# A decoder layer in fp32: five of 22 weight pieces of each half of the down projections as seven block products, and turns queued behind the weight split

## The chip, the cores and the metric

The kernel runs on one core of a Trainium2 chip. The time is device microseconds of that core, from launch to end; the measure is the median of several runs. A profile of one execution gives each instruction of the engines: TensorE (PE, and PEld for its weight loads), VectorE (DVE), ScalarE (ACT), GpSimd (POOL) and SyncE (SP), which issues most DMAs.

## The reference

One hybrid decoder layer on 256 tokens of width 2048, all in float32:

```python
def swiglu(h, w_gu, w_down):
    gate, up = jnp.split(h @ w_gu, 2, axis=-1)
    return (jax.nn.silu(gate) * up) @ w_down

x = x + 0.5 * swiglu(rmsnorm(x, ffn1_norm[l]), ffn1_w_gu[l], ffn1_w_down[l])   # D_FF = 5632
z = rmsnorm(x, mix_norm[l]) @ w_in[l]
... sliding-window attention and an HGRN2 recurrence on columns of z ...
x = x + merged @ w_out[l]
x = x + 0.5 * swiglu(rmsnorm(x, ffn2_norm[l]), ffn2_w_gu[l], ffn2_w_down[l])
```

The change bears on the two products with `w_down`, (256 x 5632) @ (5632 x 2048).

## The kernel before

**Products.** fp32 precision is made from three products of a reduced type: each operand is split into a high part (a copy to fp32r) and a low part (the rest), and hi x hi, hi x lo and lo x hi are summed. All weights stream through as *pieces* of 128 x 2048 elements (1 MB), in one list, `plan`. For each piece `load_next` issues its DMA on SP into one of four `w_raw` buffers, and `split_next` makes `w_hi` on ScalarE (line 154) and `w_lo` on VectorE (line 155) into one of two buffers each. `take` hands out piece i and first splits up to piece i + 1; a `w_hi` buffer comes free when TensorE is done with piece i - 1. A piece holds two row blocks of 128 times 1024 columns, or the like, and is used for both token halves (t = 0, 1): 8 blocks of 512 columns, each three matmuls.

**Seven products.** From group `first` on, the gate/up stage of an FFN computes two of the eight pieces of a group (`Seven.KCS = (1, 4)`) with a Strassen-like scheme: seven block products of three matmuls. It needs sums of the four weight blocks (`sums`, VectorE, lines 434 to 436, from `w_raw`), their split (`parts`: `T_hi` on ScalarE, `T_lo` on VectorE, lines 440 and 441), sums of the activation blocks (`forms`, lines 421 to 428) and two sets of four PSUM banks: `plain` takes what belongs to one output block, `summed` what is shared by several. `share` adds the shared ones up into `e`, and `outputs` adds `plain` to them. A seven-product piece needs `w_lo` for three of its four blocks only (1536 columns). The down projections are plain.

**Turns.** An activation is transposed by `send` and `fetch`: VectorE transposes 32 x 32 blocks into a block buffer (line 360), POOL's queue writes it to DRAM (line 362), and four DMAs on POOL's queue read it back with the blocks in place (line 372). Block buffers come from pool `t2` (six slots of 128 x 512); the tiles read back from `s4` (22 slots of 128 x 1024) or `t2`. `put_turned` splits a turned tile into the halves that the down projections read (`f_ah` on ScalarE, line 384; `f_al` on VectorE, line 385).

**Order.** A planner lays out each engine's queue ahead of time, in the order in which its own durations let instructions start, earlier ones in the program first; a pool's slots are given out in program order. `tc.issue_after(ins)` puts an instruction behind `ins` on the same engine. `run_gap` runs the extra work of a piece (`gaps`) with such an edge behind the newest `w_lo` (`last["rest"]`). `tick`, called twice a piece, runs the next entry of the list `deferred`, and `flush` runs what is left at a stage's end.

**Down projections.** An FFN has F = 5632 = 11 groups of 512 columns (*quads*). The output is made in two halves of 1024 columns (`cg`), each 22 pieces; quad q of the activation serves pieces 2q and 2q + 1 of both halves and is fetched three quads ahead. In piece 0 of the first half `finish_last` finishes the last gate/up group: four additions (line 507), two gated parts (519, 521), two turns. At a half's end `project_residual` adds 0.5 times the four banks to `old`, the residual, loaded earlier (line 620), and `done` stores the result and, in the first FFN, starts the next norm (`h2`). `po`, the last projection before the second FFN, does the same for `h3`. For the first two quarters, `add_later` puts into `deferred`: the squares and the turn of the quarter, eight empty entries, and two `take_back`, which multiply the turned tile by the gains (line 279) and split it.

Of the kernel before, what the change touches and what calls it, by code (L numbers as in the profile page):

```python
# [15 lines left out]
P = 128  # L16
D = 2048
S = 256
# [38 lines left out]
def tile_layer(  # L57
# [11 lines left out]
    wp = ctx.enter_context(tc.tile_pool(name="wp", bufs=2))  # L69
    hp = ctx.enter_context(tc.tile_pool(name="hp", bufs=1))  # L70
    s4p = ctx.enter_context(tc.tile_pool(name="s4p", bufs=22))
    t2p = ctx.enter_context(tc.tile_pool(name="t2p", bufs=6))
    cp = ctx.enter_context(tc.tile_pool(name="cp", bufs=1))
    sp = ctx.enter_context(tc.tile_pool(name="sp", bufs=2))
    mmp = ctx.enter_context(tc.tile_pool(name="mmp", bufs=6, space=bass.MemoryType.PSUM))
# [5 lines left out]
    def t2(name, shape=(P, 512)):  # L81
        return t2p.tile(list(shape), F32, name=name, tag="t2")
# [152 lines left out]
    class Normed:  # L235
# [31 lines left out]
        def add_later(self, q, pieces):  # L267
            turned = []

            def turn_off():  # L270
                self.squares(q, pieces)
                turned.extend([fetch(x) for x in [send(self.name, pieces[t]) for t in range(T)]])

            def take_back(t):
                k = q * 4
                x, tok = turned[t], slice(t * P, (t + 1) * P)
                h, l = (y[:, k:k + 4, tok].rearrange("p q (g c) -> p g q c", g=4) for y in (self.hi, self.lo))
                with tc.issue_after(last["copy"]), tc.issue_after(last["rest"]):
                    VE.tensor_tensor(out=x, in0=x, in1=self.g[:, k:k + 4].unsqueeze(1).unsqueeze(3)
                                     .broadcast_to([P, 4, 4, 32]), op=ALU.mult)  # L280
                    SC.copy(h, x)
                    VE.tensor_tensor(out=l, in0=x, in1=h.bitcast(F32), op=ALU.subtract)

            if q < 2:

                deferred.extend([turn_off] + [nothing] * 8 + [lambda t=t: take_back(t) for t in range(T)])
                return

            def first():
                self.squares(q, pieces)  # L290
# [15 lines left out]
        def xh(self, k):  # L306
            return self.hi[:, k, :]
# [46 lines left out]

    def send(name, nat):

        blocks = t2(f"{name}_blk", (P, 4, 4, 32))
        VE.transpose(out=blocks, in_=nat.rearrange("p (q j i) -> p j q i", q=4, j=4))  # L360
        there = tc.dram_tile([P, 512], F32, name=f"{name}_dram")
        GP.dma_start(there, blocks.rearrange("p j q c -> p (j q c)"))  # L362
        return name, there
# [38 lines left out]
    class Seven:  # L402
# [14 lines left out]
        def forms(self, p):  # L417

            k = 2 * self.KCS[p]
            A, f = t2("A", (P, 2, S)), t2("S", (P, 4, P))  # L420
            VE.tensor_tensor(out=A, in0=self.h.hi[:, k:k + 2, :].bitcast(F32),
                             in1=self.h.lo[:, k:k + 2, :].bitcast(F32), op=ALU.add)
            a11, a21, a12, a22 = (A[:, j, t * P:(t + 1) * P] for j in (1, 0) for t in range(2))
            for i, x, y, op in ((0, a21, a22, ALU.add), (1, f[:, 0], a11, ALU.subtract),
                                (2, a21, a11, ALU.subtract), (3, a12, f[:, 1], ALU.subtract)):
                VE.tensor_tensor(out=f[:, i], in0=x, in1=y, op=op)
            SC.copy(self.sh[:, p], f)
            VE.tensor_tensor(out=self.sl[:, p], in0=f, in1=self.sh[:, p].bitcast(F32), op=ALU.subtract)

        def sums(self, i):  # L430

# [8 lines left out]
                SC.copy(h, t)  # L440
                VE.tensor_tensor(out=l, in0=t, in1=h.bitcast(F32), op=ALU.subtract)  # L441

        def project(self, plain, summed, gaps):

            h = self.h
            for kc in range(KT // 2):
                hi, lo = take(f"{self.name}_gu")
                run_gap(gaps, kc)
                k = 2 * kc
                if kc not in self.KCS:  # L450
                    for t in range(T):
                        tok = slice(t * P, (t + 1) * P)
                        order = [((0, 1), [i]) for i in range(2)] if kc == KT // 2 - 1 else \
                            [([j], range(2)) for j in range(2)]
                        for js, bs in order:
                            for j in js:
                                ah, al = h.xh(k + j)[:, tok], h.xl(k + j)[:, tok]
                                st, sp_ = kc == j == 0, kc == KT // 2 - 1 and j == 1
                                cols = {i: slice(j * 1024 + i * 512, j * 1024 + i * 512 + 512) for i in bs}
                                for i in bs:  # L460
                                    mm(plain[2 * t + i], ah, hi[:, cols[i]], st, False)
                                    mm(plain[2 * t + i], ah, lo[:, cols[i]], False, False)
                                for i in bs:
                                    mm(plain[2 * t + i], al, hi[:, cols[i]], False, sp_)
                        tick()
                    continue
                p = self.KCS.index(kc)

                def a(j, t):
                    return tuple(x(k + j)[:, t * P:(t + 1) * P] for x in (h.xh, h.xl))  # L470

                def s(i):
                    return self.sh[:, p, i], self.sl[:, p, i]

                def b(i):
                    return tuple(x[:, i * 512:(i + 1) * 512] for x in (hi, lo))

                def t(i):
                    c = slice(i % 2 * 512, i % 2 * 512 + 512)
                    return self.th[i // 2][:, c], self.tl[i // 2][:, c]  # L480

                for n, (o, x, y) in enumerate((
                        (plain[0], a(0, 0), b(0)), (plain[1], s(3), b(1)), (plain[2], a(0, 1), t(3)),
                        (summed[0], a(1, 0), b(2)), (summed[1], s(0), t(1)), (summed[2], s(1), t(2)),
                        (summed[3], s(2), t(0)))):
                    st, sp_ = n > 2 and p == 0, n > 2 and p == 1
                    mm(o, x[0], y[0], st, False)
                    mm(o, x[0], y[1], False, False)
                    mm(o, x[1], y[0], False, sp_)
                    if n in (2, 6):  # L490
                        tick()
# [17 lines left out]
    def ffn(name, h, old, done, first):  # L509
# [30 lines left out]
        base = taken[0]  # L540
        for g in range(first, G):
            seven.update(base + g * 8 + kc for kc in Seven.KCS)
        sets = None
        for g in range(G):
            gaps = {kc: [] for kc in range(8)}
# [32 lines left out]
            sets = [x[1], x[0]] if (G - 1 - g) % 2 == 0 else [x[0], x[1]]  # L578
            summed = sets[1]
            gaps[5].append(lambda: sv[0].share(summed))  # L580
            sv[0].project(sets[0], summed, gaps)

        def finish_last():
            sv[0].outputs(sets[0])
            for t in range(T):
                gated_part(G - 1, t, sv[0].e[t][:, :512], sv[0].e[t][:, 512:])
                send_part(G - 1, t)

        for cg in range(2):
            gaps = {kc: [] for kc in range(2 * G)}  # L590
            if cg == 0:
                gaps[0].append(finish_last)
            for q in range(G):
                Q = cg * G + q
                gaps[2 * q].append(lambda Q=Q: fetch_quad(Q + 3))
                for t in range(T):
                    gaps[2 * q + t].append(lambda Q=Q, t=t: put_quad(Q + 1, t))

            class Side:
                xh = staticmethod(lambda k, o=4 * G * cg: act.xh(o + k))  # L600
                xl = staticmethod(lambda k, o=4 * G * cg: act.xl(o + k))

            project_residual(f"{name}_d", cg, F // P, Side, 0.5, old, done, gaps)

    def project_residual(name, cg, nk, parts, scale, old, done, gaps={}):
# [11 lines left out]
        bk = project(name, 1024, nk, parts.xh, parts.xl, fetch, gaps)  # L617
# [687 lines left out]
```

## Time and the profile before

| | |
|---|---|
| median of 3 runs | 2081.43 us (2080.98, 2081.43, 2084.72) |
| profiled execution: time, span | 2085.7 us, 2083.9 us |
| busy: PE, PEld, DVE, ACT, POOL | 2069.9, 1709.2, 1396.1, 987.3, 306.7 us |
| matmuls (PE instructions) | 9369 |
| HBM read | 428.21 MB, 217 GB/s read and written over the span |

The profile's times are measured from the span's first instruction. Matmuls overlap in the records, so PE's busy time is an upper view of its work. A row of a timeline has the start, the duration of the merged instructions, the engine, the line, the operation and, in brackets, the idle time before it and what ended it.

### The profile page before, as it was taken

How to read it: one execution, taken by the hardware profiler on the slowest of the kernel's cores; microseconds unless marked ns; L12 is line 12 of the kernel's file. 1: busy time of each engine (PE TensorE's matmuls, PEld its weight loads, DVE VectorE, ACT ScalarE, POOL GpSimd, SP SyncE). 2: the span in 40 equal slices, each digit the busy share in tenths (PEclk: the TensorE clock that was granted, in tenths of full speed). 3: DMA queues.
4: the chain of work that ended last, by engine and by line, in shares of the span. 5: the costliest groups of instructions: out<-in, count | busy, mean ns of one | idle time of the engine just before them, and what ended most of it. 6: DMA issues, size and time to landing. Idle time of an engine off the chain costs nothing.

```text
span 2083.9 us, 24269 instructions
## 1 busy us (share of the span) xinstructions
PE 2069.9 (99%) x9369; PEld 1709.2 (82%) x9369; DVE 1396.1 (67%) x1344; ACT 987.3 (47%) x894; POOL 306.7 (15%) x550
## 2 busy tenths in 40 slices
PE   9999999999999999999999999999999999999999
PEld 7888888888878888878787888888888888888887
DVE  4877888886556565555576555567888788765554
ACT  5544444444445454444455533445444444544443
POOL 0011000014515000033120000101110000046400
PEclk9999999999999999999999999999999999999999
DMA  8576656668869665567354555776665666689963
GB/s 286 191 237 231 218 193 212 218 217 271 266 229 280 223 209 179 185 226 235 133 207 166 191 185 183 237 244 222 221 227 198 216 210 218 209 263 291 274 212 116
DMA packets 180122, 454.74 MB, mean 218 GB/s; under 512 B 18771, under 2 KB 21542, under 8 KB 180006
## 3 DMA queue, kind: packets, MB, share of 16 engines
q1 hardware_dynamic: 155830, 397.57, 56.5%
q0 software_dynamic: 20400, 48.79, 7.7%
q10 hardware_dynamic: 3776, 6.83, 1.0%
q8 instruction: 73, 1.20, 0.2%
q14 instruction: 43, 0.35, 0.0%
HBM read 428.21 MB, written 24.91 MB: 217 GB/s over the span
## 4 chain that ended last, share of the span: by engine, by line
PE 84%; issue 12%; DMA 2%; DVE 1%; ACT 0%; POOL 0%; POOLq 0%; DVEq 0%; ACTq 0%
PE P L94 38%; PE f_d L94 18%; PE f_gu L94 6%; PE zbA L94 4%; PE po L94 4%; PE zbR L94 4%; PE zgo L94 2%; PE pa L94 2%; PE pr L94 2%; DMA f_a_T<-f_a_dram 1%; DVE w_lo L155 1%; DMA h_T<-h_dram 1%; PE pv_ps L94 0%; PE o_ps L94 0%; PE s_ps L94 0%
## 5 line engine op out<-in xcount | busy, mean ns | idle before, releaser
L155 DVE TENSOR_TENSOR w_lo<-w_raw,w_hi 128x2048 fp32r<-128x2048 f32 (+2 forms) x374 | 826.4, 2211 | 579.2 <-ACT w_hi L154 578.8
L154 ACT CAST w_hi<-w_raw 128x2048 fp32r<-128x2048 f32 (+2 forms) x374 | 691.3, 1850 | 808.9 <-PE f_d L94 224.5
L94 PE MATMUL P<-w_lo,h_hi 128*128 128x512 f32 x988 | 384.2, 389 | 0.5 <-DVE w_lo L155 0.5
L94 PE MATMUL P<-w_hi,h_hi 128*128 128x512 f32 x988 | 383.9, 389 | 0.0
L94 PE MATMUL P<-w_hi,h_lo 128*128 128x512 f32 x988 | 322.7, 389 | 0.0
L94 PE MATMUL f_d<-w_lo,f_ah 128*128 128x512 f32 x704 | 274.7, 390 | 2.6 <-DVE w_lo L155 2.6
L94 PE MATMUL f_d<-w_hi,f_ah 128*128 128x512 f32 x704 | 274.7, 390 | 0.0
L94 PE MATMUL f_d<-w_hi,f_al 128*128 128x512 f32 x704 | 220.0, 390 | 0.0
L94 PEld LDWEIGHTS P<-w_lo,h_hi 128*128 128x128 f32 x988 | 185.4, 188 | 39.4 <-DVE w_lo L155 0.9
L94 PEld LDWEIGHTS P<-w_hi,h_lo 128*128 128x128 f32 x988 | 185.5, 188 | 38.4
L94 PEld LDWEIGHTS P<-w_hi,h_hi 128*128 128x128 f32 x988 | 185.5, 188 | 38.4
L372 POOL DMA_DIRECT2D f_a_T<-f_a_dram x352 | 191.6, 549 | 135.7 <-DMA f_a_T<-f_a_dram 51.0
L94 PEld LDWEIGHTS f_d<-w_lo,f_ah 128*128 128x128 f32 x704 | 132.6, 188 | 30.8 <-DVE w_lo L155 3.0
L94 PEld LDWEIGHTS f_d<-w_hi,f_ah 128*128 128x128 f32 x704 | 132.6, 188 | 27.4
L94 PEld LDWEIGHTS f_d<-w_hi,f_al 128*128 128x128 f32 x704 | 132.5, 188 | 27.5
L440 ACT CAST T_hi<-T 128x1024 fp32r<-128x1024 f32 x76 | 79.6, 1048 | 141.6 <-DVE T L434 140.0
L362 POOL DMA_DIRECT2D f_a_dram<-f_a_blk x44 | 24.3, 553 | 811.3 <-DVE f_a_blk L360 808.2
L441 DVE TENSOR_TENSOR T_lo<-T,T_hi 128x1024 fp32r<-128x1024 f32 x76 | 89.6, 1218 | 0.0
L94 PE MATMUL f_gu<-w_hi,h_hi 128*128 128x512 f32 x192 | 75.9, 397 | 0.7 <-ACT w_hi L154 0.7
L94 PE MATMUL f_gu<-w_lo,h_hi 128*128 128x512 f32 x192 | 74.8, 390 | 0.0
L94 PE MATMUL f_gu<-w_hi,h_lo 128*128 128x512 f32 x192 | 61.5, 390 | 0.0
L385 DVE TENSOR_TENSOR f_al<-f_a_T,f_ah 128x512 fp32r<-128x512 f32 x88 | 60.2, 684 | 0.0
(318 smaller groups left out, 2854.2 us busy)
## 6 DMA issues: line engine op xcount, KB each, us to landing
w_raw<-in_ffn_w_gu SPq DMA_DIRECT2D x350, 512.0 KB, 4.3
w_raw<-in_ffn_w_down SPq DMA_DIRECT2D x88, 1024.0 KB, 6.3
w_raw<-in_w_in SPq DMA_DIRECT2D x74, 1024.0 KB, 4.9
f_a_T<-f_a_dram POOLq DMA_DIRECT2D x352, 64.0 KB, 6.1
w_raw<-in_w_out SPq DMA_DIRECT2D x16, 1024.0 KB, 4.8
f_a_dram<-f_a_blk POOLq DMA_DIRECT2D x44, 256.0 KB, 5.3
w_raw<-in_w_attn_branch SPq DMA_DIRECT2D x8, 1024.0 KB, 4.8
w_raw<-in_w_hg_branch SPq DMA_DIRECT2D x8, 1024.0 KB, 4.8
```

The lines of the kernel that those rows point to most:

```text
L94: last["mm"] = PE.matmul(o, lhsT=lhsT, rhs=rhs, start=start, stop=stop).ins
L154: last["copy"] = SC.copy(hi[:, c], raw[:, c]).ins
L155: last["rest"] = VE.tensor_tensor(out=lo[:, c], in0=raw[:, c], in1=hi[:, c].bitcast(F32), op=ALU.subtract).ins
L362: GP.dma_start(there, blocks.rearrange("p j q c -> p (j q c)"))
L372: GP.dma_start(res[j * 32:(j + 1) * 32].rearrange("p g q c -> p g (q c)"), v[j])
L385: VE.tensor_tensor(out=l, in0=turned, in1=h.bitcast(F32), op=ALU.subtract)
L440: SC.copy(h, t)
L441: VE.tensor_tensor(out=l, in0=t, in1=h.bitcast(F32), op=ALU.subtract)
```

## The change

Pieces 3, 7, 11, 15 and 19 of the 22 of each half are computed as seven products. The forms come from the turned quad (`turned_forms`, a tile `Sd` in `s4`), three pieces ahead; `sums` two and `parts` one piece ahead. The two halves swap the roles of two sets of four banks, and the halves' ends are new: `share` in piece 20, `add_shared` (0.5 x shared + old, four VectorE instructions) in piece 21, and four final additions after it. `Seven.project` gets its operands as arguments. In `send` the block transpose is placed behind the newest `w_lo`, for every turn of the kernel; the blocks and turned tiles of `h2` and `h3` come from `s4`, and `t2` has seven slots.

```diff
-    t2p = ctx.enter_context(tc.tile_pool(name="t2p", bufs=6))
+    t2p = ctx.enter_context(tc.tile_pool(name="t2p", bufs=7))
@@ Normed.add_later
             def turn_off():
                 self.squares(q, pieces)
-                turned.extend([fetch(x) for x in [send(self.name, pieces[t]) for t in range(T)]])
+
+                blk, back = (s4(f"{self.name}_{n}", F32, (P, T, 4, 4, 32)) for n in ("blk", "T"))
+                there = [send(self.name, pieces[t], blk[:, t]) for t in range(T)]
+                turned.extend([fetch(x, back[:, t]) for t, x in enumerate(there)])
@@
-    def send(name, nat):
-
-        blocks = t2(f"{name}_blk", (P, 4, 4, 32))
-        VE.transpose(out=blocks, in_=nat.rearrange("p (q j i) -> p j q i", q=4, j=4))
+    def send(name, nat, blocks=None):
+
+        blocks = t2(f"{name}_blk", (P, 4, 4, 32)) if blocks is None else blocks
+        with tc.issue_after(last["rest"]):
+            VE.transpose(out=blocks, in_=nat.rearrange("p (q j i) -> p j q i", q=4, j=4))
@@ class Seven
+        def add_forms(self, a11, a21, a12, a22, hi, lo, view):
+            f = t2("S", (P, 4, P))
+            for i, x, y, op in ((0, a21, a22, ALU.add), (1, view(f[:, 0]), a11, ALU.subtract),
+                                (2, a21, a11, ALU.subtract), (3, a12, view(f[:, 1]), ALU.subtract)):
+                VE.tensor_tensor(out=view(f[:, i]), in0=x, in1=y, op=op)
+            SC.copy(hi, f)
+            VE.tensor_tensor(out=lo, in0=f, in1=hi.bitcast(F32), op=ALU.subtract)
+
+        def turned_forms(self, x, j):
+
+            r = s4("Sd", F32R, (P, 2, 4, P))
+            a11, a21, a12, a22 = (x[:, t, :, i, :] for i in (j + 1, j) for t in range(2))
+            self.add_forms(a11, a21, a12, a22, r[:, 0], r[:, 1], lambda y: y.rearrange("p (g c) -> p g c", g=4))
+            return r[:, 0], r[:, 1]
@@ ffn
+        KCD = range(3, 2 * G, 4)
+        for cg in range(2):
+            seven.update(base + G * 8 + cg * 2 * G + kc for kc in KCD)
...
+        last_plain = sets[0]
+        x = [bank("P") for _ in range(6)] + [trb("P") for _ in range(2)]
+        sets = [x[:4], x[4:]]
+        forms = {}
+
+        def make_forms(cg, kc):
+            forms[cg, kc] = sv[0].turned_forms(there[cg * G + kc // 2], 2 * (kc % 2))
 
         for cg in range(2):
             gaps = {kc: [] for kc in range(2 * G)}
             if cg == 0:
                 gaps[0].append(finish_last)
+            for kc in KCD:
+                gaps[kc - 3].append(lambda cg=cg, kc=kc: make_forms(cg, kc))
+                gaps[kc - 2].append(lambda i=base + G * 8 + cg * 2 * G + kc: sv[0].sums(i))
+                gaps[kc - 1].append(lambda: sv[0].parts())
             for q in range(G):
                 Q = cg * G + q
                 gaps[2 * q].append(lambda Q=Q: fetch_quad(Q + 3))
                 for t in range(T):
                     gaps[2 * q + t].append(lambda Q=Q, t=t: put_quad(Q + 1, t))
-            project_residual(f"{name}_d", cg, F // P, Side, 0.5, old, done, gaps)
+            plain, summed = sets[cg], sets[1 - cg]
+            res = []
...
+            def add_shared():
+                for t in range(T):
+                    for i in range(2):
+                        VE.scalar_tensor_tensor(out=res[i][t], in0=sv[0].e[t][:, i * 512:(i + 1) * 512], scalar=0.5,
+                                                in1=res[i][t], op0=ALU.mult, op1=ALU.add)
+
+            gaps[2 * G - 2].append(lambda: sv[0].share(summed))
+            gaps[2 * G - 1].append(add_shared)
+            sv[0].project(f"{name}_d", F // P, list(KCD), lambda k: act.xh(4 * G * cg + k),
+                          lambda k: act.xl(4 * G * cg + k), lambda kc: forms[cg, kc], plain, summed, gaps, fetch_old)
+            flush()
+            for t in range(T):
+                for i in range(2):
+                    VE.scalar_tensor_tensor(out=res[i][t], in0=plain[2 * t + i], scalar=0.5, in1=res[i][t],
+                                            op0=ALU.mult, op1=ALU.add)
+            for i in range(2):
+                done(cg * 2 + i, res[i])
```

`fetch_old` (left out) loads `old` as before, ahead of piece 19.

## Rows read from the trace of the kernel before

**Rows 1.** The page, busy time, share of the span, instructions.
```profile
PE 2069.9 (99%) x9369; PEld 1709.2 (82%) x9369; DVE 1396.1 (67%) x1344; ACT 987.3 (47%) x894; POOL 306.7 (15%) x550
```
**Rows 2.** The chain by time: start, duration, work.
```profile
618.89 15.07 PE f_d L94 x59
...
925.65 45.96 PE zgo L94 x191
...
1373.17 5.44 PE f_gu L94 x24
...
1840.22 239.44 PE f_d L94 x1056
```
**Rows 3.** Windows: busy time of each engine, granted clock, DMA share, GB/s.
```profile
611.00:630.00 19.00, 16.39 (x66) 13.05 (x65) 8.29 (x6) 8.16 (x10) 11.54 (x22) 0.91 0.80 240
...
921.00:971.00 50.00, 46.31 (x195) 37.84 (x193) 23.24 (x13) 23.99 (x24) 29.41 (x54) 0.93 0.85 279
...
1418.00:1840.00 422.00, 422.00 (x1863) 349.57 (x1862) 336.72 (x295) 200.13 (x151) 29.51 (x54) 1.00 0.64 217
```
**Rows 4.** TensorE's waits: total us, times, longest.
```profile
PE zgo L94 <- DVE w_lo L155: 3.7, 1, 3.7
PE f_d L94 <- DVE w_lo L155: 2.6, 1, 2.6
...
PE P L94 <- DVE w_lo L155: 0.5, 1, 0.5
```
**Rows 5.** VectorE's timeline, second half of the first FFN.
```profile
615.95 0.71 DVE L360 STREAM_TRANSPOSE h_blk<-old 128x512 f32<-128x512 f32 x1 [5.24 <-DMA h_dram<-h_blk]
```
**Rows 6.** VectorE's timeline, start of `zgo`.
```profile
922.00 1.43 DVE L360 STREAM_TRANSPOSE q0T_blk<-q 128x512 f32<-128x512 f32 x2 [4.17 <-DMA kT_dram<-kT_blk]
```
**Rows 7.** VectorE's groups by line and form: busy us, mean ns, idle before.
```profile
L155 DVE TENSOR_TENSOR w_lo<-w_raw,w_hi 128x2048 fp32r<-128x2048 f32 x330 | 754.9, 2288 | 555.4 <-ACT w_hi L154 555.1
L441 DVE TENSOR_TENSOR T_lo<-T,T_hi 128x1024 fp32r<-128x1024 f32 x76 | 89.6, 1218 | 0.0
L155 DVE TENSOR_TENSOR w_lo<-w_raw,w_hi 128x1536 fp32r<-128x1536 f32 x38 | 66.6, 1753 | 23.7 <-ACT w_hi L154 23.7
L385 DVE TENSOR_TENSOR f_al<-f_a_T,f_ah 128x512 fp32r<-128x512 f32 x88 | 60.2, 684 | 0.0
...
L434 DVE TENSOR_TENSOR T<-w_raw 128x1024 f32<-128x1024 f32 x38 | 45.7, 1202 | 0.0
...
L436 DVE TENSOR_TENSOR T<-w_raw,T 128x512 f32<-128x512 f32 x38 | 26.3, 692 | 1.3
...
L620 DVE SCALAR_TENSOR_TENSOR old<-f_d,old 128x512 f32<-128x512 f32 x16 | 10.6, 686 | 11.1 <-PE f_d L94 11.1
...
L426 DVE TENSOR_TENSOR S<-A 128x128 f32<-128x128 f32 x8 | 2.0, 288 | 0.1
```
**Rows 8.** VectorE's timeline, start of the second FFN's down projections.
```profile
1842.20 2.29 DVE L155 TENSOR_TENSOR w_lo<-w_raw,w_hi 128x2048 fp32r<-128x2048 f32 x1 [2.55 <-ACT w_hi L154]
1844.41 2.48 DVE L507 TENSOR_TENSOR E<-P,E 128x512 f32<-128x512 f32 x4
...
1848.70 2.25 DVE L155 TENSOR_TENSOR w_lo<-w_raw,w_hi 128x2048 fp32r<-128x2048 f32 x1
```
**Rows 9.** VectorE's timeline, last `po` project and start of `f_gu`.
```profile
1336.57 0.71 DVE L360 STREAM_TRANSPOSE h_blk<-old 128x512 f32<-128x512 f32 x1 [1.26 <-DMA x<-old]
...
1358.87 2.29 DVE L155 TENSOR_TENSOR w_lo<-w_raw,w_hi 128x2048 fp32r<-128x2048 f32 x1 [1.21 <-ACT w_hi L154]
...
1371.96 1.29 DVE L279 TENSOR_TENSOR h_T<-h_T,gains 128x512 f32<-128x512 f32 x2
...
1376.32 2.29 DVE L155 TENSOR_TENSOR w_lo<-w_raw,w_hi 128x2048 fp32r<-128x2048 f32 x1
```
**Rows 10.** POOL's timeline in `po`; landing times of the `h_T` fetches there.
```profile
1338.80 4.36 POOL L372 DMA_DIRECT2D h_T<-h_dram x8 [6.36 <-DMA h_dram<-h_blk]
...
DMA to landing us min/median/max: 4.2/7.1/7.8
```

More of the change, by code (lines that the diff above doesn't have):

```diff
@@ L419, in forms @@
             k = 2 * self.KCS[p]
-            A, f = t2("A", (P, 2, S)), t2("S", (P, 4, P))
+            A = t2("A", (P, 2, S))
             VE.tensor_tensor(out=A, in0=self.h.hi[:, k:k + 2, :].bitcast(F32),
@@ L423, in forms @@
             a11, a21, a12, a22 = (A[:, j, t * P:(t + 1) * P] for j in (1, 0) for t in range(2))
[L424 to L428, printed above, removed]
+            self.add_forms(a11, a21, a12, a22, self.sh[:, p], self.sl[:, p], lambda x: x)
+        def add_forms(self, a11, a21, a12, a22, hi, lo, view):
[10 more added lines that the diff above has]
+            return r[:, 0], r[:, 1]
         def sums(self, i):
@@ L441, in parts, with project @@
                 VE.tensor_tensor(out=l, in0=t, in1=h.bitcast(F32), op=ALU.subtract)
[L443 to L447, printed above, removed]
+        def project(self, name, nk, kcs, xh, xl, forms, plain, summed, gaps, near_end=None):
+            end = nk // 2 - 1
+            for kc in range(nk // 2):
+                hi, lo = take(name)
                 run_gap(gaps, kc)
                 k = 2 * kc
-                if kc not in self.KCS:
+                if kc == end - 2 and near_end is not None:
+                    near_end()
+                if kc not in kcs:
                     for t in range(T):
                         tok = slice(t * P, (t + 1) * P)
-                        order = [((0, 1), [i]) for i in range(2)] if kc == KT // 2 - 1 else \
+                        order = [((0, 1), [i]) for i in range(2)] if kc == end else \
                             [([j], range(2)) for j in range(2)]
@@ L456, in project @@
                             for j in js:
-                                ah, al = h.xh(k + j)[:, tok], h.xl(k + j)[:, tok]
-                                st, sp_ = kc == j == 0, kc == KT // 2 - 1 and j == 1
+                                ah, al = xh(k + j)[:, tok], xl(k + j)[:, tok]
+                                st, sp_ = kc == j == 0, kc == end and j == 1
                                 cols = {i: slice(j * 1024 + i * 512, j * 1024 + i * 512 + 512) for i in bs}
@@ L466, in project @@
                     continue
-                p = self.KCS.index(kc)
                 def a(j, t):
-                    return tuple(x(k + j)[:, t * P:(t + 1) * P] for x in (h.xh, h.xl))
+                    return tuple(x(k + j)[:, t * P:(t + 1) * P] for x in (xh, xl))
                 def s(i):
-                    return self.sh[:, p, i], self.sl[:, p, i]
+                    return tuple(x[:, i] for x in forms(kc))
                 def b(i):
@@ L485, in project @@
                         (summed[3], s(2), t(0)))):
-                    st, sp_ = n > 2 and p == 0, n > 2 and p == 1
+                    st, sp_ = n > 2 and kc == kcs[0], n > 2 and kc == kcs[-1]
                     mm(o, x[0], y[0], st, False)
@@ L580, in ffn @@
             gaps[5].append(lambda: sv[0].share(summed))
-            sv[0].project(sets[0], summed, gaps)
+            sv[0].project(f"{name}_gu", KT, Seven.KCS, h.xh, h.xl,
+                          lambda kc: [x[:, Seven.KCS.index(kc)] for x in (sv[0].sh, sv[0].sl)],
+                          sets[0], summed, gaps)
         def finish_last():
-            sv[0].outputs(sets[0])
+            sv[0].outputs(last_plain)
             for t in range(T):
@@ L597, in ffn, with fetch_old, project_residual @@
                     gaps[2 * q + t].append(lambda Q=Q, t=t: put_quad(Q + 1, t))
-            class Side:
-                xh = staticmethod(lambda k, o=4 * G * cg: act.xh(o + k))
-                xl = staticmethod(lambda k, o=4 * G * cg: act.xl(o + k))
-            project_residual(f"{name}_d", cg, F // P, Side, 0.5, old, done, gaps)
-    def project_residual(name, cg, nk, parts, scale, old, done, gaps={}):
+            plain, summed = sets[cg], sets[1 - cg]
+            res = []
+            def fetch_old():
+                for i in range(2):
+                    q = cg * 2 + i
+                    res.append([])
+                    for t in range(T):
+                        o = t2("old")
+                        nc.sync.dma_start(o, old[t * P:(t + 1) * P, q * 512:(q + 1) * 512])
+                        res[i].append(o)
+            def add_shared():
[8 more added lines that the diff above has]
+            flush()
+            for t in range(T):
+                for i in range(2):
+                    VE.scalar_tensor_tensor(out=res[i][t], in0=plain[2 * t + i], scalar=0.5, in1=res[i][t],
+                                            op0=ALU.mult, op1=ALU.add)
+            for i in range(2):
+                done(cg * 2 + i, res[i])
+    def project_residual(name, cg, nk, parts, scale, old, done):
         res = []
@@ L615, in fetch @@
                     res[i].append(o)
-        bk = project(name, 1024, nk, parts.xh, parts.xl, fetch, gaps)
+        bk = project(name, 1024, nk, parts.xh, parts.xl, fetch)
         for t in range(T):
```

## The prediction

> **What bounds the kernel now.** I read the page's busy shares first, then the chain by time and the windows, then TensorE's waits, and only then the timelines around the places that the change touches. TensorE is busy 99% of the span [rows 1], and that share alone says little, because matmuls overlap in it. The chain says more: in the second FFN's down projections 1056 matmuls start one after another in 239.44 us [rows 2], 0.2267 us each, and the gate/up stage before it passes 1863 in 422.0 us, again 0.2265 each [rows 3]. In that stage two of eight weight pieces already run as seven products; those products cost what any matmul costs, and nothing waits there. So nearly everywhere the time is the number of 512-column matmuls times 0.2267 us: a matmul taken out is worth that much as long as VectorE, which makes the low halves and the sums, keeps ahead.
>
> It doesn't keep ahead in two places [rows 4]: the first `zgo` piece waits 3.7 us for `w_lo`, and one down piece of the first FFN 2.6 us. Each has a tail: the granted clock is 0.91 and 0.93 in those windows instead of 1.00 [rows 3]. In the chain the 59 matmuls after the `f_d` wait take 15.07 us, 1.7 more than 59 x 0.2267, and the 191 after the `zgo` wait 45.96 us, 2.6 more [rows 2]. The waits thus cost 2.6 + 1.7 = 4.3 us and 3.7 + 2.6 = 6.3 us. Both have one cause. A turn's block transpose (L360) stands in VectorE's queue ahead of a split's `w_lo` and waits for its `t2` slot, held by an earlier block whose send is still under way: 5.24 us at 615.95 [rows 5], 4.17 us at 922.00 [rows 6].
>
> **The matmuls removed.** A plain piece is 8 block products of three matmuls, 24; a piece as seven products is 21. Five pieces in each of two halves in two FFNs are 20 pieces: 60 matmuls x 0.2267 = 13.6 us. I take it whole; the lower end, with each piece losing its three in waits, is nothing.
>
> **The two old waits.** Inside `send` the transpose now gets an edge behind the newest split that is traced, so the turn of h2's second quarter can no longer run far ahead of its place in the program, in front of a `w_lo`; h2's blocks also leave the `t2` slots. The same edge spreads the twelve `kT`, `qT`, `q0T` turns over the ticks at which they are traced, two a piece of 5.44 us, and `t2` has a seventh slot. I take back both waits, 4.3 + 6.3 = 10.6 us. The bounds are 0 (the pile-up of sends on POOL merely moves later) and 10.6.
>
> **What VectorE gets instead.** Per group of four down pieces its work is, by the means of one [rows 7]: three splits 2.288 and one of 1536 columns 1.753; four `f_al` 0.684; `sums` 1.202 + two of 0.69; two `T_lo` 1.218; four form additions 0.288 and the form's low part, of `f_al`'s shape, 0.68. That is 8.6 + 2.7 + 2.6 + 2.4 + 1.8 = 18.2 us in (3 x 24 + 21) x 0.2267 = 21.1 us, 86%. The gate/up stage carries 336.7 us in 422, 80%, without a wait [rows 3]. In the steady run of a half I therefore put the added work at nothing; what hides it is three full pieces of matmuls. How tight it is shows in the piece ahead of a seven-product one: its cast ends some 2.5 us in (the 2.0 us of [rows 8], and half a microsecond for a `T_hi` copy that goes first), the split of 1536 columns follows until 4.2, two `T_lo` until 6.5. The eighth matmul of the seven-product piece, the first to read the second `T_lo`, is due at 5.44 + 7 x 0.2267 = 7.0. The margin is 0.5 us, and 20 pieces depend on it.
>
> The starts of the halves have no such cover. In the first half `finish_last` shares piece 0 with the forms for piece 3, and `sums` comes in piece 1. VectorE's first split can begin only 2.0 us into the half, at 1842.20 [rows 8]. Up to the second `T_lo` it must do three splits (6.3), four `outputs` additions (2.48 [rows 8]), two gated parts and two turns (estimated 0.7 each by the other 512-column rows, 2.8), forms (1.8), two `f_al` (1.4), `sums` (2.6) and two `T_lo` (2.4): 19.8 us. The rows shown overlap their successors by some 0.07 us (2.29 us at 1842.20, the next at 1844.41 [rows 8]), so about 18.4 net, done at 1860.6. Piece 3 starts at 1840.2 + 3 x 5.44 = 1856.5 and wants the low part at its eighth matmul, 1858.1. It is 2.5 us late, 2.7 with the shorter wait for the split itself counted. That happens in both FFNs: 5.4 us. Would the clock fall too? It did after the 2.6 us wait; the trace has none of 1 to 2 us that would tell for two shorter ones. I add half of the 1.7 us tail to each: 7.1 us. Bounds: 0, if VectorE's order puts the turns last, and 2 x (2.7 + 1.7) = 8.8.
>
> At the second half's start the four `add_shared` and four final additions (0.686 each [rows 7], 0.62 back to back) stand ahead of its piece-1 split. The split before them runs, as in rows 8, from 2.0 to 4.2 us into piece 21, so until 1.2 us ahead of the half. Four additions bring VectorE to 1.3 us in, an `f_al` to 1.9, the final four to 4.4, the split to 6.6; wanted is it at 5.44 + 0.23 = 5.67: 0.9 us late. In the first FFN two transposes more make it about 1.7. Together 2.7; bounds 0 and 5.
>
> **The turn before the second gate/up.** Here the new edge costs. h3's second quarter is turned off in the twelfth tick of the last `po` project. Today its transposes run far ahead of that place, one at 1336.57 [rows 9]. With the edge they stand behind the split of 1358.87, which ends near 1361.1; one `h_T` product goes first, so they finish near 1363.0. Two sends are issued until 1364.1. The fetches started 6.36 us after the sends before, eight in 4.36 us, and landed after 4.2 to 7.8 us, median 7.1 [rows 10]. So the first tile lands near 1379.2, the second near 1381.4. Both are multiplied by the gains when the project's leftover work is flushed, at 1371.96 today [rows 9], and the split for the second `f_gu` piece stands behind them, now at 1376.32. `f_gu` starts at 1373.17 [rows 2] and wants that split 25 matmuls later, 1378.8. Late next are this split, TensorE behind it, and ScalarE, which has the next cast queued. With one product ahead the split runs 1379.6 + 0.2 to 1382, 3 us late; with both ahead 6 us. At the price of the old waits (4.3 for 2.6) that is 5 or 10 us. Bounds 0 and 10; I take 5: the product that is up first is the likelier to stand ahead of the split, the other can go on either side of it.
>
> The Trainium skill (DMA: Bandwidth & Descriptors, Latency and other measured facts) puts a transfer's fixed cost at about 2 us. By that figure both tiles would be there near 1372 to 1374, this term would be nothing and the forecast 5 us lower. The trace does not agree for these transfers: 6.4 and 7.1 us.
>
> POOL's queue gets no new DMA. On SP the `old` loads move to piece 16 or later of their half; they are wanted in piece 21, five pieces or 27 us on. The `s4` slots hold eight tiles of `Seven` longer; with three or four turned quads, four to six halves of `act`, one or two forms and h2's blocks I count 18 to 22 of 22, so I put slots at nothing, with a short wait as bound, covered by the fetch's lead of three quads (32 us).
>
> **Sum.** -13.6 - 10.6 + 7.1 + 2.7 + 5.0 = -9.4 us. The profiled execution took 2085.7 us (span 2083.9), so it would take 2076.3. The runs' median is 2081.43, 4.3 lower, with one run at 2084.72; from the median the sum gives 2072.0.
>
> **Rivals.** *The h3 turn lands in time.* Were both of its legs as quick as the quickest fetch, 4.2 us [rows 10], the fetches would begin near 1368, the last be issued at 1372 and land at 1376, and the split would start about where it does today. The term of 5 goes: 2067.0, or 2063 to 2071 with the other terms' spread. Against it: the median is 7.1. Chance 0.13. (The Trainium skill's figure for a transfer, named above, leads to this case.)
>
> *The order hides the backlog.* VectorE's queue is laid out ahead of time; if the turns, gated parts and h3 products go behind the splits, 7.1 and 5.0 shrink to 0 to 3. For it: a split stands today at 1848.70, between the two gated parts [rows 8]. Against it: most of the 18.4 us is needed work. Result 2057 to 2065; chance 0.15.
>
> *The waits move instead of going.* The h3 turn costs 10, the starts 8.8 and 2.7, and half of the 10.6 comes back because ScalarE holds its casts behind copies of late `q0T` fetches: -13.6 - 5.3 + 8.8 + 2.7 + 10 = +2.6, 2084. Between that and my case: 2076 to 2084; chance 0.22.
>
> *Slower: `T_lo` late in every seven-product piece.* Its margin is 0.5 us. If in each the `T_lo` runs behind an `f_al` and a form's low part that waits for ScalarE's copy, the piece stalls. At 9.4 / 20 = 0.47 us a piece my gain is gone; 0.7 us is 14 us in 20 pieces, and 2086. Against it: the gate/up stage, at 80%, shows 0.5 us of such waits in all [rows 4]. Chance 0.08.
>
> **Chances.** My case, one h3 product ahead of the split and the starts as worked out, gives 2068 to 2076: 0.42. Measurements of this kernel can tell about 0.2%, 4.2 us, from no change, so faster means below 2077.3: my case and the first two rivals, 0.70, and a third of the one whose waits move, 0.07; together 0.77. Same is the rest of that one, 0.15; slower 0.08. The range, 2058 to 2080, takes in all but the lowest of the hidden backlog and the middle of the moved waits.
>
> **What would show it.** Each FFN's down projections should have 1026 matmuls in place of 1056 and end 30 x 0.2267 = 6.8 us sooner, but for their waits. `zgo` and the h2 turn should wait for nothing, with the clock at 1.00 there. TensorE's waits should name `w_lo` or `T_lo` in pieces 2 to 4 of the first halves, piece 1 of the second, and `f_gu` just after `po`, with `h_T` before it on VectorE. I am wrong if `h_T` lands before its product is up, if `T_lo` ends waits through a whole half, or if the old `zgo` wait is still there.

## The result, and the profile after

The change made the kernel slower: 2097.48 us (median of four runs, 2093.80 to 2099.64) against 2081.39 for the kernel before beside it; the ratio is 1.0064, 95% interval 1.0047 to 1.0081. Forecast were 2072.0 us and a range of 2058 to 2080. The profiled execution took 2096.44 us, its span is 2094.7, 10.8 us more than before. The medians are 16.1 us apart: the profiled execution of the kernel before lay 4.3 us above its median, and some 5 us of the measured loss are in neither trace.

The page of the changed kernel, against [rows 1]: 60 matmuls fewer, as worked out, and 130 us more of VectorE.

```profile
PE 2063.8 (99%) x9309; PEld 1699.3 (81%) x9309; DVE 1526.0 (73%) x1576; ACT 1031.2 (49%) x958; POOL 305.8 (15%) x550
```

TensorE's waits in it (total us, times, longest), against [rows 4]. Neither old wait is there. Four new ones are, none of which names `T_lo`.

```profile
PE P L94 <- ACT Sd L435: 10.7, 2, 5.3
PE f_gu L94 <- DVE old L676: 4.7, 1, 4.7
PE P L94 <- DVE f_al L389: 3.8, 2, 2.2
PE zbA L94 <- DVE go L871: 3.5, 1, 3.5
...
PE P L94 <- DVE w_lo L155: 0.5, 1, 0.5
```

Windows of the changed kernel, columns as in [rows 3]. `zgo` (921 to 971) runs at a clock of 1.00 where it had 0.93, and the steady gate/up stage is as before. The four windows around the waits for `Sd`, `go` and `old` show 0.72 to 0.86.

```profile
490.70:505.00 14.30, 8.97 (x30) 6.95 (x30) 10.43 (x16) 6.03 (x8) 10.11 (x19) 0.76 0.81 250
...
921.00:971.00 50.00, 50.00 (x221) 41.03 (x220) 26.71 (x19) 23.14 (x23) 32.64 (x60) 1.00 0.96 309
968.00:980.00 12.00, 8.49 (x36) 6.81 (x35) 4.25 (x8) 7.36 (x9) 3.57 (x7) 0.86 0.51 139
1375.00:1392.00 17.00, 12.32 (x49) 9.68 (x48) 7.97 (x11) 7.62 (x13) 3.13 (x6) 0.80 0.62 190
1418.00:1840.00 422.00, 422.00 (x1864) 349.42 (x1863) 339.59 (x299) 202.84 (x153) 24.06 (x44) 1.00 0.65 217
1860.00:1872.00 12.00, 6.67 (x22) 4.94 (x21) 10.98 (x17) 5.55 (x7) 8.14 (x15) 0.72 0.87 265
```

Its chain by time has two long runs in the second FFN's down projections where [rows 2] have one: 441 matmuls in 102.00 us, 2.0 more than 441 x 0.2267, and 485 in 110.26, 0.3 more.

```profile
1866.08 102.00 PE P L94 x441
...
1979.99 110.26 PE P L94 x485
```

Cutting both traces at the first matmul of each stage shows where the 10.8 us are. Each entry is the time from the first matmul of a stage to the first of the next (f2 down: to the start of its last matmul of `w_hi` and `f_ah`), in one profiled execution of each kernel. The kernels of the experiments stand in the same table; their ratios are medians against the kernel before on the same chip, with 95% intervals.

| kernel | f1 down | zgo | zbA | f2 gate/up | f2 down | ratio |
|---|---|---|---|---|---|---|
| before | 243.9 | 49.9 | 116.0 | 467.1 | 238.7 | 1 |
| the change | 246.8 | 43.8 | 121.9 | 474.4 | 239.7 | 1.0064 (1.0047 to 1.0081) |
| e1 forms after the split | 240.0 | 43.8 | 123.4 | 472.4 | 234.1 | 1.0000 (0.999 to 1.001) |
| e2 small slots for h | 242.4 | 43.8 | 123.7 | 473.8 | 240.4 | 1.0046 (1.0031 to 1.0061) |
| e3 no edge | 247.0 | 48.3 | 116.0 | 467.1 | 240.3 | 1.0028 (1.0017 to 1.0039) |
| e4 turns only, plain down | 239.4 | 43.8 | 119.8 | 473.3 | 238.7 | 1.0020 (1.0009 to 1.003) |
| e5 = e1 + e2 | 235.9 | 43.8 | 122.8 | 476.2 | 234.2 | 0.9986 (0.9976 to 0.9995) |
| e6 = e5, h3 without edge | 235.9 | 43.8 | 120.0 | 467.1 | 234.2 | 0.9953 (0.9938 to 0.9968) |
| e7 = e6, later q0T copies | 235.9 | 43.8 | 116.1 | 467.1 | 234.1 | 0.9917 (0.9902 to 0.9932) |
| e8 = e5, 20 large slots | 235.8 | 43.8 | 121.6 | 476.0 | 234.0 | 0.9984 (0.9974 to 0.9993) |
| e9 = e1, h in a pool of its own | 236.0 | 43.8 | 121.1 | 475.2 | 234.2 | 0.9973 (0.9962 to 0.9983) |
| e10 seven products only | 235.4 | 49.1 | 116.1 | 467.0 | 234.3 | 0.9945 (0.993 to 0.996) |

Ratios in the text below have their intervals here, and line numbers differ by some lines from kernel to kernel. `zbA` and the second gate/up differ by up to 4 us between kernels whose edits don't touch them (119.8 to 123.7 and 472.4 to 476.2 with the edge). The change against before: +2.9, -6.1, +5.9, +7.3 and +1.0, with 0.5 less in `zbR` together 10.5 of the 10.8 us. The down projections got 6.8 us of matmuls less each, and not one of the two became shorter.

### The profile page after: what moved, and what is told of

It is laid out like the page before. It is cut to its first block, busy times and chain, and to the rows that moved or that the text cites. A ratio compares the mean times of both kernels' runs of the same rounds, so it can differ in the third digit from the quotient of the medians.

```text
span 2094.7 us, 24469 instructions
## 1 busy us (share of the span) xinstructions
PE 2063.8 (99%) x9309; PEld 1699.3 (81%) x9309; DVE 1526.0 (73%) x1576; ACT 1031.2 (49%) x958; POOL 305.8 (15%) x550
## 5 line engine op out<-in xcount | busy, mean ns | idle before, releaser
L155 DVE TENSOR_TENSOR w_lo<-w_raw,w_hi 128x2048 fp32r<-128x2048 f32 (+2 forms) x374 | 815.6, 2182 | 461.1 <-ACT w_hi L154 460.3
L94 PE MATMUL P<-w_hi,f_ah 128*128 128x512 f32 x584 | 228.3, 393 | 0.3 <-ACT f_ah L388 0.3
L94 PE MATMUL P<-w_lo,f_ah 128*128 128x512 f32 x584 | 228.2, 392 | 0.3
L455 ACT CAST T_hi<-T 128x1024 fp32r<-128x1024 f32 x116 | 121.6, 1048 | 186.4 <-DVE T L449 178.7
L94 PE MATMUL P<-w_hi,f_al 128*128 128x512 f32 x584 | 186.8, 391 | 3.8 <-DVE f_al L389 3.8
L456 DVE TENSOR_TENSOR T_lo<-T,T_hi 128x1024 fp32r<-128x1024 f32 x116 | 136.9, 1218 | 0.0
L94 PEld LDWEIGHTS P<-w_hi,f_al 128*128 128x128 f32 x584 | 110.1, 189 | 27.5 <-DVE f_al L389 4.7
L94 PEld LDWEIGHTS P<-w_hi,f_ah 128*128 128x128 f32 x584 | 110.5, 189 | 24.5 <-ACT f_ah L388 1.6
L94 PEld LDWEIGHTS P<-w_lo,f_ah 128*128 128x128 f32 x584 | 110.4, 189 | 24.5 <-DVE w_lo L155 1.5
L449 DVE TENSOR_TENSOR T<-w_raw 128x1024 f32<-128x1024 f32 x58 | 70.0, 1206 | 0.0
```

The lines of the kernel that those rows point to most:

```text
L94: last["mm"] = PE.matmul(o, lhsT=lhsT, rhs=rhs, start=start, stop=stop).ins
L155: last["rest"] = VE.tensor_tensor(out=lo[:, c], in0=raw[:, c], in1=hi[:, c].bitcast(F32), op=ALU.subtract).ins
L449: VE.tensor_tensor(out=t31, in0=v[:, 3:4].broadcast_to([P, 2, 512]), in1=v[:, 1:3], op=ALU.subtract)
```

## The experiments

**e1: the forms asked for after the split of the quad.** In the changed kernel TensorE stops at piece 2 of both first halves. TensorE's timeline there (a row has the start, the duration, the work and, in brackets, the idle time before it and what ended it):

```profile
490.29 0.61 PE L94 MATMUL P<-w_hi,f_al 128*128 128x512 f32 x2
496.24 0.80 PE L94 MATMUL P<-T_hi,Sd 128*128 128x512 f32 x1 [5.33 <-ACT Sd L435]
496.83 0.72 PE L94 MATMUL P<-w_hi,f_ah 128*128 128x512 f32 x1
```

and ScalarE's:

```profile
490.99 1.47 ACT L154 CAST w_hi<-w_raw 128x1536 fp32r<-128x1536 f32 x1 [2.90 <-issue]
492.37 1.04 ACT L455 CAST T_hi<-T 128x1024 fp32r<-128x1024 f32 x1
494.62 1.04 ACT L455 CAST T_hi<-T 128x1024 fp32r<-128x1024 f32 x1 [1.21 <-DVE T L451]
495.57 0.61 ACT L435 CAST Sd<-S 128x512 fp32r<-128x512 f32 x1
496.09 1.66 ACT L388 CAST f_ah<-f_a_T 128x512 fp32r<-128x512 f32 x3
```

The form is of piece 3, but one of its products stands in TensorE's queue ahead of all of piece 2, and on ScalarE the casts `f_ah` that piece 2 needs stand behind the form's. The edit moves four lines:

```diff
-            for kc in KCD:
-                gaps[kc - 3].append(lambda cg=cg, kc=kc: make_forms(cg, kc))
-                gaps[kc - 2].append(lambda i=base + G * 8 + cg * 2 * G + kc: sv[0].sums(i))
-                gaps[kc - 1].append(lambda: sv[0].parts())
             for q in range(G):
...
                     gaps[2 * q + t].append(lambda Q=Q, t=t: put_quad(Q + 1, t))
+            for kc in KCD:
+                gaps[kc - 3].append(lambda cg=cg, kc=kc: make_forms(cg, kc))
+                gaps[kc - 2].append(lambda i=base + G * 8 + cg * 2 * G + kc: sv[0].sums(i))
+                gaps[kc - 1].append(lambda: sv[0].parts())
```

> The change with one thing moved: in a piece of the down projections the forms are asked for after the split of the same quad, not ahead of it. The 5.3 us that TensorE waits for Sd in piece 2 of both first halves, with about 2 us of slow clock behind each, would then be order: the forms and the casts f_ah of quad 1 stand in the wrong order behind the turns. Theory of order: both waits go, f_ah of quad 1 is cast again some 8 us before its piece, and the time falls by 2 x 7.3 = 14.6 us to about 2083. Rival, too much VectorE work at the start of a half: the wait only moves on to T_lo or Sd in piece 3, the 2.7 us of the prediction in each FFN with a tail, and the time falls by 2 x 3 to 4 us, to about 2090.

Measured: 2084.07 us, ratio 1.0000. Both `Sd` waits are gone, and the two down projections take 6.8 and 5.6 us less. On e1's ScalarE `f_ah` is cast early again:

```profile
483.06 0.61 ACT L388 CAST f_ah<-f_a_T 128x512 fp32r<-128x512 f32 x1
...
488.54 0.62 ACT L388 CAST f_ah<-f_a_T 128x512 fp32r<-128x512 f32 x1
...
496.52 0.61 ACT L435 CAST Sd<-S 128x512 fp32r<-128x512 f32 x1
```

So it was order, worth 12.4 us. The rival, a wait of 2.7 us that moves on to piece 3, came as some 1.4 us a half. VectorE is as late as the prediction worked out: in e1 the second first half starts at 1843.5 and the two `T_lo` end at 1864.55, 21.0 us in, where 20.4 was worked out. But TensorE's queue takes the products with `w_hi` and `w_lo` first, and the first matmul that reads a `T_lo` starts 20.4 us into the half, not 17.9. e1's VectorE, then its TensorE:

```profile
1862.19 2.36 DVE L456 TENSOR_TENSOR T_lo<-T,T_hi 128x1024 fp32r<-128x1024 f32 x2
```

```profile
1863.06 0.50 PE L94 MATMUL P<-T_hi,f_ah 128*128 128x512 f32 x1 [0.21 <-ACT T_hi L455]
...
1863.86 0.39 PE L94 MATMUL P<-T_lo,Sd 128*128 128x512 f32 x1
...
1866.81 0.74 PE L94 MATMUL P<-w_lo,f_ah 128*128 128x512 f32 x2 [0.50 <-DVE w_lo L155]
```

What VectorE's backlog costs is little more than the 0.21 and 0.50 us in brackets: by the starts of the matmuls around the two waits, 1.3 us in this half (0.55 and 0.78), and 1.4 in the first FFN's.

**e2, e8 and e9: why the first FFN's second half waits.** There `f_al` ends two waits of the changed kernel. ScalarE and TensorE at the first of them, and two rows of POOL:

```profile
623.23 1.92 ACT L154 CAST w_hi<-w_raw 128x2048 fp32r<-128x2048 f32 x1 [0.30 <-PE P L94]
625.05 1.13 ACT L388 CAST f_ah<-f_a_T 128x512 fp32r<-128x512 f32 x2
```

```profile
628.46 0.73 PE L94 MATMUL P<-w_hi,f_al 128*128 128x512 f32 x2 [1.54 <-DVE f_al L389]
```

```profile
570.47 4.33 POOL L376 DMA_DIRECT2D f_a_T<-f_a_dram  x8 [3.84 <-PE P L94]
...
617.18 0.56 POOL L366 DMA_DIRECT2D h_dram<-h_blk  x1 [29.47 <-DVE h_blk L364]
```

POOL stands for 29.5 us at a send of h2 whose block isn't there, and later fetches stand behind it. That is not what makes the casts late. By count (a quad has eight fetches and two casts), the casts at 625.05 are of the quad that was fetched at 570.47, and those ahead of the second wait (648.79) are of one whose last fetch was issued at 630.5. At 625.05 ScalarE did not wait either: the casts stand in its queue behind the `w_hi` of a later piece, where the planner put them. Nor does a stand of POOL go with lost time. It is longer in e2, where the `f_al` waits are 0.7 us, and in the kernel before, which has none:

```profile
612.00 0.56 POOL L363 DMA_DIRECT2D h_dram<-h_blk  x1 [37.34 <-DVE S L431]
```

```profile
601.89 0.56 POOL L362 DMA_DIRECT2D h_dram<-h_blk  x1 [42.39 <-DVE h_blk L360]
```

e2 puts h2's and h3's tiles back:

```diff
-                blk, back = (s4(f"{self.name}_{n}", F32, (P, T, 4, 4, 32)) for n in ("blk", "T"))
-                there = [send(self.name, pieces[t], blk[:, t]) for t in range(T)]
-                turned.extend([fetch(x, back[:, t]) for t, x in enumerate(there)])
+                turned.extend([fetch(x) for x in [send(self.name, pieces[t]) for t in range(T)]])
```

> The change with the blocks and the turned tiles of h2 and h3 back in the 128 x 512 slots (t2, seven of them) and out of the 128 x 1024 slots (s4); the edge in send stays. Theory of slots: the 22 large slots run out in the second half of the first FFN, where Seven keeps eight and h2's blocks two more, so the casts f_ah of the next quad come two pieces late; with h2 out of them the f_al and f_ah waits there (1.5 + 2.3 + 0.3 us in the rows, 6.8 us of lost time in that half) go: about 2091. The h3 wait ahead of the second gate/up (7.4 us) stays, as it is the edge's. Rival, the edge or VectorE's load makes f_ah late: the half stays 6 to 7 us too long, 2095 to 2100. Against both: the old wait of h2's turn for a small slot may come back, 4.3 us.

Measured: 2093.80 us, ratio 1.0046. The first FFN's down projections are 4.4 us shorter, the `f_al` waits shrink from 3.8 to 0.7 us, and h2's old wait does not come back. With e1's edit as well (e5):

> Two mends at once: forms asked for after the split of the quad, and h2's and h3's blocks and turned tiles in the 512-column slots. If the two causes are apart, the gains add: the first FFN's down projections, 246.8 us in the change, 240.0 with the forms moved and 242.4 with the small slots, take 246.8 - 6.8 - 4.4 = 235.6, and the time is some 4.5 us below the kernel with the forms moved alone: a ratio to before of 0.998. Rival: both mends remove the same wait, and nothing is gained over the better one (1.000).

Measured: 2080.53 us, 0.9986. The first FFN's down projections take 235.9, as added up. Was it a lack of large slots? e8 takes two away, `s4p` with 20 in place of 22:

> As the run with both mends, with 20 large slots in place of 22: the two that h2's tiles took in the change are taken away, though h2 no longer uses them. Theory of slots: the waits for f_ah and f_al come back without h2, now in all four halves of the down projections, 2 to 5 us each; 8 to 20 us over the run with both mends. Rival, it was h2's own work (its additions, transfers or its place in the queues) that made f_ah late: the down projections stay as in that run, and only small losses elsewhere (0 to 3 us).

Measured: 2081.07 us, 0.9984, and 235.8 and 234.0 in the down projections: no wait came back. So the other tiles get by with 20 slots. That 22 are too few with h2's four tiles (two a quarter) among them is not ruled out by this. e9 keeps the large tiles but takes them from another pool:

```diff
-    s4p = ctx.enter_context(tc.tile_pool(name="s4p", bufs=22))
+    s4p = ctx.enter_context(tc.tile_pool(name="s4p", bufs=20))
+    h4p = ctx.enter_context(tc.tile_pool(name="h4p", bufs=2))
...
-                blk, back = (s4(f"{self.name}_{n}", F32, (P, T, 4, 4, 32)) for n in ("blk", "T"))
+                blk, back = (h4p.tile([P, T, 4, 4, 32], F32, name=f"{self.name}_{n}", tag="h4") for n in ("blk", "T"))
```

> As the run with the forms moved (large tiles for h2 and h3), but those tiles come from a pool of their own with two large slots, and the shared pool keeps 20. Sizes and memory are the same; only the line in which the tiles wait for a slot is parted. Theory of the shared line: the h2 tiles and the halves of act hold each other up in program order; apart, the second half of the first FFN's down projections loses its f_ah and f_al waits, and the two halves take 235.9 us as with small slots, against 240.0: ratio to before 0.998 to 0.999. Rival, the size: one tile for both token halves (its fetch waits for both sends) makes it late, whichever pool it is from: 240.0 stays, ratio 1.000.

Measured: 2078.78 us, 0.9973, and 236.0. Both casts of the quad of the first wait, in e1 and then in e9, whose second half starts at about the same time (its additions begin at 598.47 and 598.11):

```profile
620.18 1.13 ACT L388 CAST f_ah<-f_a_T 128x512 fp32r<-128x512 f32 x2
```

```profile
611.55 0.62 ACT L389 CAST f_ah<-f_a_T 128x512 fp32r<-128x512 f32 x1
...
618.38 0.61 ACT L389 CAST f_ah<-f_a_T 128x512 fp32r<-128x512 f32 x1
```

The total of slots and the size of the tiles are as in e1; parting the pools is enough. That the halves of `act` get their slots late because they come behind h2's tiles in the shared line fits this, but no run shows which tile stood behind which, and a larger shared pool was not run.

**e3 and e4: the edge.** e3 takes it out of `send`, and e4 is the kernel before with the edge, the large tiles and the seventh small slot, but plain down projections.

```diff
-        with tc.issue_after(last["rest"]):
-            VE.transpose(out=blocks, in_=nat.rearrange("p (q j i) -> p j q i", q=4, j=4))
+        VE.transpose(out=blocks, in_=nat.rearrange("p (q j i) -> p j q i", q=4, j=4))
```

> The change without the edge in send: block transposes may again run ahead of their place; the slots stay as in the change. Theory: the edge makes two new waits, h3's turn ahead of the second gate/up (+7.4 us against before) and zbA behind late q0T copies (+5.9), and takes away one, zgo (-6.1; its seventh small slot may take part of that away without it). So 2097.5 - 13.3 + 6.1 = 2090, or 2084 if the seventh slot is enough for zgo. The Sd and f_al waits of the down projections stay. Rival, the h3 and zbA waits come from the slots and not the edge: nothing changes there, and zgo's wait comes back: 2097 to 2104.

> The kernel before with the turns' part alone: edge in send, h2's and h3's blocks in large slots, seven small slots; the down projections stay plain. Theory of the traces: the two old waits go (-4.3 for h2, -6.1 for zgo), two new ones come (+7.4 for h3, +5.9 for zbA), the down projections show no Sd and no f_al wait: 2081.4 + 2.9, about 2084. By the prediction's terms it would be -10.6 + 5.0, about 2076. Rival, the large slots alone already crowd the second half of the first FFN: f_al waits there without any form, and 2088 or more.

Measured: e3 2090.04 us, 1.0028; e4 2087.18 us, 1.0020. In e3 `zbA` and the second gate/up are back at 116.0 and 467.1, and `zgo` takes 48.3 (its wait is 3.1 us; with six small slots, e10 below, it takes 49.1). e4 has the edge's three marks (43.8, 119.8, 473.3) without any seven products: the turns' part alone is no gain but a loss of 0.2%.

**e6: h3's turn without the edge.** In the changed kernel VectorE, POOL and TensorE show at the end of `po`:

```profile
1364.00 1.30 DVE L364 STREAM_TRANSPOSE h_blk<-old 128x512 f32<-128x512 f32 x2
...
1381.99 0.69 DVE L282 TENSOR_TENSOR h_T<-h_T,gains 128x512 f32<-128x512 f32 x1 [7.63 <-DMA h_T<-h_dram]
1382.60 1.28 DVE L676 SCALAR_TENSOR_TENSOR old<-po,old 128x512 f32<-128x512 f32 x2
```

```profile
1365.00 1.15 POOL L366 DMA_DIRECT2D h_dram<-h_blk  x2 [14.81 <-DVE h_blk L364]
1373.78 4.35 POOL L376 DMA_DIRECT2D h_T<-h_dram  x8 [7.63 <-DMA w_raw<-in_ffn_w_gu]
```

```profile
1383.34 0.79 PE L94 MATMUL f_gu<-w_hi,h_hi 128*128 128x512 f32 x1 [4.68 <-DVE old L676]
1383.93 0.63 PE L94 MATMUL f_gu<-w_lo,h_hi 128*128 128x512 f32 x1
1384.36 1.05 PE L94 MATMUL f_gu<-w_hi,h_lo 128*128 128x512 f32 x2
```

The transposes run 27 us later than in [rows 9] (25 within the stage, as the kernel is 2.3 us late here), the tile's product starts 18 us after them, and behind the product that waits for it stand the additions (L676) that empty `po`'s banks. `f_gu` writes to these banks and stops after 14 matmuls.

```diff
-        with tc.issue_after(last["rest"]):
+        def turn():
             VE.transpose(out=blocks, in_=nat.rearrange("p (q j i) -> p j q i", q=4, j=4))
+
+        if name == "h3":
+            turn()
+        else:
+            with tc.issue_after(last["rest"]):
+                turn()
```

> As the run with both mends, and h3's block transposes alone without the edge in send. Theory: the edge alone delays h3's turn, so the start of the second gate/up loses nothing more than before (from its first matmul to the first down matmul 467.1 us as before, against 472 to 474 with the edge), and the time falls by 5 to 7 us: ratio 0.995. Rival, the transfers of h3 collide with the weight stream wherever they start: the wait before f_gu stays and the ratio is 0.998.

Measured: 2075.09 us, 0.9953; the stage takes 467.1 again, and `po` gets 0.8 us longer, with a wait of 0.5 us for `w_lo`. The transfers beside the weight stream were not the cause, the edge was.

**e7: later copies of q0T.** ScalarE of the changed kernel at the end of `zgo`, and then TensorE:

```profile
969.86 0.62 ACT L974 COPY q0T<-q0T_T 128x512 f32<-128x512 f32 x1 [3.26 <-DMA q0T_T<-q0T_dram]
972.19 0.62 ACT L974 COPY q0T<-q0T_T 128x512 f32<-128x512 f32 x1 [1.71 <-DMA q0T_T<-q0T_dram]
...
974.12 1.26 ACT L870 ACTIVATE sig<-zgo,h_rstd 128x512 f32<-128x512 f32 x2
975.97 0.62 ACT L974 COPY q0T<-q0T_T 128x512 f32<-128x512 f32 x1 [0.58 <-DMA q0T_T<-q0T_dram]
```

```profile
975.65 0.80 PE L94 MATMUL zbA<-w_hi,h_hi 128*128 128x512 f32 x1 [3.51 <-DVE go L871]
976.24 0.63 PE L94 MATMUL zbA<-w_lo,h_hi 128*128 128x512 f32 x1
976.67 0.63 PE L94 MATMUL zbA<-w_hi,h_hi 128*128 128x512 f32 x1
```

The copies wait for fetches that the spread turns make late; `sig` and, on VectorE, `go`, which have to read `zgo`'s banks before `zbA` can have them, stand behind. The edit in `hgrn`:

```diff
-        for _ in range(2):
+        for _ in range(6):
             yield
         while back:
             bring()
```

> As the run before, and ScalarE's copies of the last q0T tiles asked for six steps after their last fetch in place of two, so that the four sig activations stand ahead of them in its queue. Theory: zbA waits because sig, which frees zgo's banks, stands behind copies that wait for late q0T fetches; then the 116.0 us of that stage come back from 123.5, zgo keeps its 43.8, and the time falls by 7 us more: ratio 0.991 to 0.992. Rival, the fetches themselves are the limit (HGRN work of the next pieces wants q0T): the wait moves to a later stage, and the ratio stays at 0.995.

Measured: 2067.28 us (2066.58 to 2068.05), 0.9917, the best of all: `zgo` 43.8 and `zbA` 116.1. e7's ScalarE has the four `sig` first:

```profile
956.81 2.43 ACT L873 ACTIVATE sig<-zgo,h_rstd 128x512 f32<-128x512 f32 x4
...
960.91 1.16 ACT L977 COPY q0T<-q0T_T 128x512 f32<-128x512 f32 x2
```

**e10: the seven products alone.** e1's order, no edge, six small slots, h2 and h3 in small ones.

> The kernel before with the seven products of the down projections alone (forms asked for after the quad's split): no edge in send, six small slots, h2 and h3 in small slots. If the removed matmuls are worth 0.2267 us each and the rest is independent: 13.6 us less, some 3 us of short VectorE waits in the four halves, and the two old waits of before stay (zgo 3.7, h2's turn 2.6, with their tails): 2081.4 - 10.6, a ratio of 0.995. Rival: VectorE has less room beside h2's turn than before, and its wait in the second half of the first FFN grows by several us: 0.997 or more, with that half longer than the 117 us of the second FFN's.

Measured: 2073.67 us, 0.9945; the down projections take 235.4 and 234.3, `zgo` keeps its wait of 3.7 us. h2's old wait is gone without anything of the turns' part.

## Why the prediction was wrong

*The matmuls removed, -13.6: right.* [Rows 1] against the page after: 60. With its order mended the part alone gives 0.55% (e10), with 4.5 us of it from the old h2 wait.

*The old h2 wait, -4.3: gone.* What the prediction named, the edge and the large tiles, is enough under plain projections (e4: 239.4 in place of 243.9). But the seven products alone remove it too (e10), so the turns' part was not needed for it.

*The old zgo wait, -6.3: right in its place (-6.1), wrong in the sum.* "I take back both waits" is a step that failed: `zbA` loses 5.9 us. The moved-waits rival had named this mechanism, ScalarE behind late `q0T` copies (it had its casts held; it was `sig`), and priced half of the 10.6.

*The first halves' start, +7.1: the cost is 15.2, and 12.4 of it has another cause.* By the starts of the matmuls the two stops of the changed kernel cost 7.9 and 7.3 us, tails included. The backlog was sized well (21.0 us against 20.4), but it costs TensorE only some 1.4 us a half, without a tail (e1). The step that failed put the forms among VectorE's work and never asked where `Sd` stands in the queues of TensorE and ScalarE, nor what is queued behind it.

*The second halves' start, +2.7: 0.8.* The wait that it named is there in both FFNs, 0.4 us each. In the second one, VectorE's split for piece 1 and the matmuls that read it:

```profile
1977.66 2.28 DVE L155 TENSOR_TENSOR w_lo<-w_raw,w_hi 128x2048 fp32r<-128x2048 f32 x1
```

```profile
1978.78 1.07 PE L94 MATMUL P<-w_hi,f_ah 128*128 128x512 f32 x4
1979.99 0.73 PE L94 MATMUL P<-w_lo,f_ah 128*128 128x512 f32 x2
```

What the sum did not have is the line of h2's tiles (4.0 to 4.4 us, e9 and e2). The step that failed put slots at nothing, "covered by the fetch's lead of three quads": the fetches were early enough, and late were the casts, which the lead does not cover.

*h3's turn, +5.0, bounds 0 to 10: right in cause (e6), 7.3 in size.* Late next were the additions that empty `po`'s banks, which the prediction did not name; the split that it named ends a wait of 2.4 us in e4, beside 1.7 us for the additions.

*The steady run at nothing: right.* The second FFN's second half (1967 to 2089) has no wait for VectorE but the 0.4 us just shown, and the rival of a late `T_lo` in every piece is out: no wait names it.

In sum, taken from the table: -13.6 for the matmuls - 4.5 - 6.1 + 5.9 + 12.4 + 4.2 + 7.3, which is +5.6. The four halves of e5 and e7 are 5.5 us longer than the matmuls left are worth (235.9 + 234.1, less 239.4 + 238.7 of e4 - 13.6); 2.7 of it is the backlog at the first halves' starts and 0.8 the second halves'. That makes +11.1, and with 0.5 less in `zbR` 10.6, where the traces show 10.8.

## What to carry to other kernels

Where queues are laid out ahead, a new tile is costed by three questions, asked on each engine that touches it: what stands behind its producer, which product of it is queued earliest, and whose slot it stands in line for. Extra work that fits under the matmuls stopped TensorE for 5.3 us in each first half by its place, and moving one group of lines gave 12 us back. An edge that keeps instructions from running ahead is given only to those that did harm: here one helper serves five kinds of turns; the edge took a wait of 6 us out of `zgo`, and `zbA`, behind the same turns, and the turn of h3 paid 13 for it.

## What the runs showed of the hardware

After waits of 3.5 to 5.3 us TensorE's matmuls start 0.43 us apart in place of 0.2267 for some 3 to 5 us (the rows from 1383.93 and 976.24 above), with a granted clock of 0.72 to 0.86 in these windows: the lower of its two levels, 1.2 of 2.4 GHz, for part of them. After the `f_al` waits of 1.5 and 2.2 us the matmuls of the same kernel go on 0.23 us apart. The first leg of a turn through DRAM takes 6.4 us in [rows 10]; in the changed kernel the fetches of h3 were issued 7.6 us after their sends, and the wait's releaser is named as a weight transfer. Both ran beside a stream of weights, and no run shows a turn without one.
